# One matmul of 129 columns in place of 65 and 64 in a first layer's attention, with the low part added at eviction

## The chip, the cores and the metric

The kernel runs on one NeuronCore of a Trainium2 chip. The metric is the time of one execution on the device, in microseconds (us). Every matrix product is made of float16 pieces: a float32 value is split into a high float16 part and the float16 remainder (the "low" part), and three products (high by high, high by low, low by high) are summed in PSUM.

## The reference

Two layers act on 1024 latent tokens of width 1024 and 256 context tokens. The first is grouped-query attention: 16 query heads and 4 key/value heads of width 64, keys from latents and context together (1280 of them), then a SiLU gate and an output projection. The second is attention over a neighbourhood window. The change concerns the first layer alone:

```python
s = jnp.einsum('bqkgd,bskd->bkgqs', qi, k_all).astype(jnp.float32) * ATTN_SCALE
p = jax.nn.softmax(s, axis=-1).astype(v_all.dtype)
return jnp.einsum('bkgqs,bskd->bqkgd', p, v_all)
...
yx = (o * jax.nn.silu(z)) @ w_out
```

The changed lines compute the product of `p` and `v_all`, the division by the softmax sum, and the product with the gate.

## The kernel before

**Tiling.** Tokens are cut into tiles of 128: eight of latents, two of context. Layer one goes through eight units `u`, one for each pair of heads; a unit has three groups of query tiles `pt_`: two groups of four latent tiles, and one of the two context tiles. Inside a unit, `a_proj` (L944) makes queries and gates, `a_att` (L1177) the attention with keys on the partitions, and `q_att` (L1112) another form of the attention with queries on the partitions. For units 0 to 5 (`QH`) the second head of the latent groups goes through `q_att`; all else goes through `a_att`.

**One pass of `a_att`** is one head of one group. For a latent group it loops over the ten key tiles `kt`: two matmuls (L1204, L1205) put scores of 128 keys by 512 queries into a PSUM tile `st`; ScalarE takes the exponent twice, into float16 `ph` (L1189) and float32 `pf` (L1191); `p_split` (L1058) subtracts them, mostly on GpSimd, into the low part `pl`; `pv_mm` (L1068) multiplies with the values. `pv_mm` is called three key tiles late (`flush(3)`). A context group has two key tiles and two query tiles, and its exponents are named `phc` and `plc`.

**The values** lie in `v1[:, kt, g, :]` (L720), 130 float16 elements for each key tile and value head: 64 high values, one column of a constant (its product is the softmax sum), 64 low values from element 65 on. `pv_mm` issues three matmuls for each query tile: `ph` by the 65 columns of high values and constant (L1072), `ph` by the 64 low values into the same PSUM columns (L1073), `pl` by the 65 columns (L1074). The exponent tile is the stationary operand, so each matmul has a weight load (LDWEIGHTS, engine PEld) of its own.

**Eviction.** When the last key tile of a pass is in, `o_evict` (L1047) reads the PSUM tile `pv`: a reciprocal of the sums (L1050), a product with it (L1052), a product with the gate into `og` (L1054), all three on VectorE. `pv` has two buffers under one tag, which `q_att` uses for its `qpv` too: in units 0 to 5, `a_att` goes from pass to pass on one buffer while `q_att` holds the other. A pass can start its value matmuls only when its buffer has been read to the end.

**The order of the work** is not that of the code. `Planner` (L50) takes the recorded instructions with their dependences, prices each (`cost`, L93: a 65-column matmul at 30, a 64-column one at 34, longer ones at columns / 2.4 + 3), and places them engine by engine (`schedule`). `refine` (L468) repeats this with due times from the last order and keeps the order whose planned end is earliest. The orders of all engines are then fixed. An edit anywhere in layer one therefore moves instructions around it on every engine.

Of the kernel before, what the change touches and what calls it, by code (L numbers as in the profile page):

```python
# [16 lines left out]
ALU = mybir.AluOpType  # L17
# [4 lines left out]
P = 128  # L22
# [4 lines left out]
NT = NX + NC  # L27
TOK = NT * P
HD = 64
NH = 16  # L30
NKV = 4
EPS = 1e-6
# [477 lines left out]
def trunk_kernel(ctx, tc, x, cx, cc, ng_row, w_mod, w_mod0, b_mod, a_qz, a_kv, a_qg, a_kg, a_w_out,  # L510
                 b_in, tab, b_w_out, fin_g, ones, cos_t, sin_t, out):
    nc = tc.nc
    V, S, G, T, DM = nc.vector, nc.scalar, nc.gpsimd, nc.tensor, nc.sync
# [8 lines left out]
    def ps_tag(name, tag, dt=F32, shape=(P, 512)):  # L522
        return (psum if tag in ("pj", "pv") else psum1).tile(list(shape), dt, name=name, tag=tag, bufs=2)
# [8 lines left out]
        return ps_tag(name, "st")  # L532

    def ps_pv(name):
        return ps_tag(name, "pv", shape=(P, 4, 65))

    idf = main.tile([P, P], F32, name="idf")
    make_identity(nc, idf)
# [183 lines left out]
    G.memset(v1[:, :, :, 64:65], 2.0 * WS * WS)  # L722
    gcq = ap.tile([P, NX, HD], F32, name="gcq")
    gsq = ap.tile([P, NX, HD], F32, name="gsq")
    gcol = ap.tile([P, HD], F32, name="gq")
    gks = ap.tile([P, HD], F32, name="gk")

# [5 lines left out]
    def sq_tiles(pool):  # L733

        ts = [pool.tile([P, 4, HD + 1], F32, name=f"sq{j}", bufs=1) for j in range(2)]
        for s_ in ts:
            G.memset(s_[:, :, HD:HD + 1], HD * EPS * WS * WS)
        return ts
# [121 lines left out]
    for kt in range(KT):  # L860
# [8 lines left out]
        for t in ((0, 2) if kt < 2 else (0,)):  # L869
            n = 2 if kt < 2 else 4  # L870
# [56 lines left out]
    aq = apool2.enter_context(tc.tile_pool(name="aq", bufs=2))  # L927
    NPAIR = NH // 2

# [116 lines left out]

    def o_evict(pool, pv, og, n, sz, t0, i, nm):  # L1047

        rs = pool.tile([P, 4], F32, name="ors" + nm, tag="ors", bufs=2)
        V.reciprocal(rs[:, 0:n], pv[:, 0:n, 64])  # L1050
        hd = slice(i * HD, (i + 1) * HD)
        V.tensor_tensor(pv[:, 0:n, 0:HD], pv[:, 0:n, 0:HD], rs[:, 0:n].unsqueeze(2).broadcast_to([P, n, HD]),  # L1052
                        op=ALU.mult)
        V.tensor_tensor(og[:, 0:n, hd], pv[:, 0:n, 0:HD], sz[:, t0:t0 + n, hd], op=ALU.mult)  # L1054

    nsplit = [0]

# [10 lines left out]
    def pv_mm(pv, hi, lo, v, n, first, last):  # L1068

        for t in range(n):  # L1070
            c = slice(t * P, (t + 1) * P)
            T.matmul(pv[:, t, :], hi[:, c], v[:, 0:65], start=first and t == 0, stop=False)  # L1072
            T.matmul(pv[:, t, 0:HD], hi[:, c], v[:, 65:129], start=False, stop=False)  # L1073
            T.matmul(pv[:, t, :], lo[:, c], v[:, 0:65], start=False, stop=last and t == n - 1)  # L1074

    def o_out(pool, og, n, dst, u, nm):

# [99 lines left out]
    def a_att(u, pt_):  # L1177
# [18 lines left out]
        og = og_of(u, pt_)  # L1196
        for i in ((0,) if pt_ < 2 and u in QH else (0, 1)):
            pvs = ps_pv(f"pv{u}{i}{pt_}")
            if pt_ < 2:
                for kt in range(NT):  # L1200
                    st = ps_st(f"st{u}{i}{pt_}{kt}")
                    kc = slice(kt * P, (kt + 1) * P)
                    so = st.rearrange("p (t q) -> p t q", q=P)
                    T.matmul(so, k1[:, g, kc], q1[:, :, i, :], start=True, stop=False)  # L1204
                    T.matmul(so, k2[0:65, g, kc], q2[0:65, :, i, :], start=False, stop=True)  # L1205
                    ph, pl = p_tiles(st, f"{u}{i}{pt_}{kt}")
                    pend.append(lambda pvs=pvs, ph=ph, pl=pl, kt=kt: pv_mm(
                        pvs, ph, pl, v1[:, kt, g, :], 4, kt == 0, kt == NT - 1))
                    flush(3)
                    yield 800  # L1210
            else:
                st = ps_st(f"stc{u}{i}")
                for j in range(2):
                    kc = slice((NX + j) * P, (NX + j + 1) * P)
                    o = st[:, j * 256:(j + 1) * 256].rearrange("p (t q) -> p t q", q=P)
                    T.matmul(o, k1[:, g, kc], q1[:, :, i, :], start=True, stop=False)
                    T.matmul(o, k2[0:65, g, kc], q2[0:65, :, i, :], start=False, stop=True)
                ph, pl = p_tiles(st, f"c{u}{i}")

                def cpv(pvs=pvs, ph=ph, pl=pl):  # L1220
                    for j in range(2):
                        c = slice(j * 256, (j + 1) * 256)
                        pv_mm(pvs, ph[:, c], pl[:, c], v1[:, NX + j, g, :], 2, j == 0, j == 1)
                pend.append(cpv)
                yield 800

            def fin(pvs=pvs, i=i):
                o_evict(aq, pvs, og, n, sz, 0, i, f"{u}{i}{pt_}")
                og_done(u, pt_)
# [18 lines left out]
    first = 1.0  # L1248
# [102 lines left out]
    for t in range(4):  # L1351
        v = OV + OW * t
# [519 lines left out]
def _bias(rpb):  # L1872

    rp = np.pad(rpb.transpose(0, 2, 1), ((0, 0), (0, 0), (8, 8)))
    t = np.full((NH, P, 9, 8, GR), NEG, np.float32)
    t[:, :, 4:8] = 0.0
    for p in range(P):
# [7 lines left out]
        t[:, p, 3, 0:c, k] = v[:, 16:16 + c]  # L1885
    return t.reshape(NH, P, 9 * P)

# [54 lines left out]
```

## Time and profile before

| what | value |
|---|---|
| time, median of 3 runs | 1319.07 us (1318.21 to 1323.93) |
| profiled execution, its own time | 1312.96 us |
| span in that profile | 1311.2 us |
| granted TensorE clock | 0.999 |
| attention of layer one | about 130 to 690 us of the span |
| output projection of layer one begins | about 690 us |

A PE row is a matmul, a PEld row its weight load. Matmuls overlap in the records: a 65-column matmul is shown with about 193 ns, while the next one starts some 30 ns after it. The price of a matmul in a stream is therefore read from start to start, not from its duration.

### The profile page before, as it was taken

What the parts mean: (1) busy time and instruction counts of PE and PEld (TensorE: products, weight loads), DVE (VectorE), ACT (ScalarE), POOL (GpSimd) and SP (SyncE); (2) the same over time, 40 slices, a digit from 0 to 9 for tenths busy, and PEclk for the clock granted to TensorE, in tenths of its full rate; (3) what the DMA queues carried; (4) which work ended last, traced back from release to release, by engine and by line L of the source; (5) the groups of instructions that cost most, each with busy time, mean ns of one, the idle gap of its engine ahead of it and who ended that gap; (6) DMA issues with size and microseconds to landing.
All of it is one profiled execution on the core that took longest, in us unless ns stands there. A gap on an engine that the chain in (4) does not pass through costs nothing. (4 is left out here: it accounts for less than half of the span.)

```text
span 1311.2 us, 37092 instructions
## 1 busy us (share of the span) xinstructions
PE 1281.5 (98%) x14503; PEld 899.9 (69%) x14503; DVE 1025.2 (78%) x2410; ACT 893.9 (68%) x1835; POOL 807.4 (62%) x1030
## 2 busy tenths in 40 slices
PE   9999999999999999999999999999999999999997
PEld 6458777777777777767654466778696777868543
DVE  4787788798979798969658896778888788788743
ACT  3672797788878887778864345777878677777611
POOL 1572787677687876768864883556665555553432
PEclk9999999999999999999999999999999999999999
DMA  9422478778788886884406795789798887979923
GB/s 371 162 82 72 99 142 167 134 179 170 140 161 184 153 164 145 168 213 124 137 34 181 209 165 175 136 172 182 148 182 167 165 188 138 195 155 236 244 97 113
DMA packets 431610, 211.40 MB, mean 161 GB/s; under 512 B 386697, under 2 KB 390601, under 8 KB 431433
## 3 DMA queue, kind: packets, MB, share of 16 engines
q1 hardware_dynamic: 431434, 209.04, 71.4%
q8 instruction: 113, 1.85, 0.6%
q14 instruction: 63, 0.52, 0.1%
HBM read 97.23 MB, written 14.71 MB: 85 GB/s over the span
## 5 line engine op out<-in xcount | busy, mean ns | idle before, releaser
L1066 POOL TENSOR_TENSOR pl<-pf,ph 128x256 f16<-128x256 f32 x340 | 239.4, 728 | 66.6 <-ACT pf L1191 51.8
L1066 POOL TENSOR_TENSOR bph<-bpf,bph 128x256 f16<-128x256 f32 (+1 forms) x172 | 148.9, 890 | 184.4 <-ACT bpf L1640 122.9
L967 PE MATMUL pa<-wa,x 128*128 128x256 f16 x1536 | 216.5, 272 | 0.4 <-DVE mrow L626 0.2
L967 PEld LDWEIGHTS <-x 128*128 128x128 f16 x1536 | 141.8, 97 | 35.6 <-issue 1.8
L1189 ACT ACTIVATE ph<-st 128x512 f16<-128x512 f32 x200 | 118.7, 605 | 64.0 <-PE st L1205 53.3
L998 DVE TENSOR_REDUCE mxp<-pm 128x1 f32<-128x512 f32 x160 | 107.7, 683 | 14.6 <-PE pm L997 13.0
L1191 ACT ACTIVATE pf<-st 128x512 f32<-128x512 f32 x200 | 119.0, 610 | 0.2 <-POOL pl L1066 0.2
L1066 POOL TENSOR_TENSOR qpp<-qpf,qpp 128x512 f16<-128x512 f32 x84 | 96.4, 1168 | 30.0 <-ACT qpf L1148 23.2
L1639 ACT ACTIVATE bph<-bpf,bnx 128x640 f16<-128x640 f32 (+1 forms) x128 | 96.4, 794 | 26.6 <-DVE bnx L1634 25.9
L1505 PEld LDWEIGHTS <-wb 128*128 128x128 f16 x672 | 61.3, 98 | 68.1 <-issue 4.9
L1073 PE MATMUL pv<-v,ph 128*128 128x64 f16 x800 | 104.7, 195 | 0.0
L1072 PE MATMUL pv<-v,ph 128*128 128x65 f16 x800 | 104.1, 193 | 0.0
L1074 PE MATMUL pv<-v,pl 128*128 128x65 f16 x800 | 103.5, 192 | 0.1
L1640 ACT ACTIVATE bpf<-bpf,bnx 128x640 f32<-128x640 f32 (+1 forms) x128 | 101.3, 792 | 0.2
L1503 PEld LDWEIGHTS <-s 128*128 128x128 f16 x1536 | 87.0, 98 | 4.9 <-issue 3.7
L1072 PEld LDWEIGHTS <-ph 128*128 128x128 f16 x800 | 75.9, 97 | 19.9 <-issue 0.5
L1073 PEld LDWEIGHTS <-ph 128*128 128x128 f16 x800 | 75.5, 97 | 13.8 <-issue 0.2
L1074 PEld LDWEIGHTS <-pl 128*128 128x128 f16 x800 | 76.2, 99 | 9.4 <-POOL pl L1066 0.8
L1204 PE MATMUL st<-q,k 128*128 128x512 f16 x200 | 75.4, 379 | 3.8 <-ACT pf L1191 3.6
L1205 PE MATMUL st<-q,k 65*128 65x512 f16 x200 | 74.9, 380 | 3.1 <-DMA q<-zt 3.0
L1468 POOL TENSOR_TENSOR tsb<-wsb 128x256 f32<-128x256 f32 x64 | 52.5, 841 | 31.2 <-DMA wsb<-in_b_in 23.3
L1140 DVE CUSTOM_DVE_ANT_0 qpf<-qs,zero 128x512 f32<-128x512 f32 x96 | 65.6, 684 | 6.0 <-PE qs L1138 2.7
(549 smaller groups left out, 3889.4 us busy)
## 6 DMA issues: line engine op xcount, KB each, us to landing
wg<-in_w_mod SPq DMA_DIRECT2D x64, 256.0 KB
wsb<-in_b_in SPq DMA_DIRECT2D x64, 256.0 KB
tb<-in_tab SPq DMA_DIRECT2D x16, 576.0 KB
wm<-in_w_mod SPq DMA_DIRECT2D x16, 512.0 KB
wsa<-in_a_qz SPq DMA_DIRECT2D x32, 256.0 KB
xstage<-in_x SPq DMA_DIRECT2D x8, 512.0 KB
wsoa<-in_a_w_out SPq DMA_DIRECT2D x16, 256.0 KB
x<-in_x SPq DMA_DIRECT2D x8, 512.0 KB
```

The source lines that it names most:

```text
L967: T.matmul(ps[:, :, i, :], hA(a, kt, t), wt[w][:, kt, :], start=n == 0, stop=n == 3 * KT - 1)
L998: V.tensor_reduce(mxs[i][:, t, ch:ch + 1], pm, axis=AX.X, op=ALU.max)
L1066: G.tensor_tensor(lo[:, c], p32[:, c], hi[:, c], op=ALU.subtract)
L1072: T.matmul(pv[:, t, :], hi[:, c], v[:, 0:65], start=first and t == 0, stop=False)
L1073: T.matmul(pv[:, t, 0:HD], hi[:, c], v[:, 65:129], start=False, stop=False)
L1074: T.matmul(pv[:, t, :], lo[:, c], v[:, 0:65], start=False, stop=last and t == n - 1)
L1189: S.activation(ph, st, AF.Exp)
L1191: S.activation(p32, st, AF.Exp)
L1204: T.matmul(so, k1[:, g, kc], q1[:, :, i, :], start=True, stop=False)
L1503: T.matmul(ps[:, t], a_blk(a, kt, m)[:, t], w[kt][:, b, WIX[m]], start=f, stop=l, skip_group_check=not first)
L1639: S.activation(ph, pf[:, 0:k_], AF.Exp, bias=m)
L1640: S.activation(pf[:, 0:k_], pf[:, 0:k_], AF.Exp, bias=m, accum_out=sums[:, t - t0, i:i + 1])
```

## The change

Columns of `pv` are laid out anew: each query tile gets `VC` = 129 columns, in the order of `v1` (64 high, 1 sum, 64 low), as far as the bank of 512 columns goes. That holds three tiles of 129 and a fourth of 65. For the first three query tiles, one matmul of 129 columns replaces the pair of 65 and 64, and the product with the low values lands in columns of its own. The fourth tile keeps its three matmuls. Context groups have two query tiles, and both take the new form. At eviction ScalarE copies the low columns into `og`, VectorE adds them to the high ones in PSUM, and then the two products follow as before. `refine` gets 10 rounds for 5.

```diff
+VC = 2 * HD + 1
...
-        return ps_tag(name, "pv", shape=(P, 4, 65))
+        return ps_tag(name, "pv")
...
+        def cols(c, k, m):
+            a = pv[:, c:c + m]
+            return bass.AP(a.tensor, a.offset, [list(a.ap)[0], [VC, k], [1, m]])
+
         rs = pool.tile([P, 4], F32, name="ors" + nm, tag="ors", bufs=2)
-        V.reciprocal(rs[:, 0:n], pv[:, 0:n, 64])
-        hd = slice(i * HD, (i + 1) * HD)
-        V.tensor_tensor(pv[:, 0:n, 0:HD], pv[:, 0:n, 0:HD], rs[:, 0:n].unsqueeze(2).broadcast_to([P, n, HD]),
-                        op=ALU.mult)
-        V.tensor_tensor(og[:, 0:n, hd], pv[:, 0:n, 0:HD], sz[:, t0:t0 + n, hd], op=ALU.mult)
+        V.reciprocal(rs[:, 0:n].unsqueeze(2), cols(HD, n, 1))
+        hd, w = slice(i * HD, (i + 1) * HD), min(n, 3)
+        S.copy(og[:, 0:w, hd], cols(HD + 1, w, HD))
+        V.tensor_tensor(cols(0, w, HD), cols(0, w, HD), og[:, 0:w, hd], op=ALU.add)
+        o = cols(0, n, HD)
+        V.tensor_tensor(o, o, rs[:, 0:n].unsqueeze(2).broadcast_to([P, n, HD]), op=ALU.mult)
+        V.tensor_tensor(og[:, 0:n, hd], o, sz[:, t0:t0 + n, hd], op=ALU.mult)
...
-            c = slice(t * P, (t + 1) * P)
-            T.matmul(pv[:, t, :], hi[:, c], v[:, 0:65], start=first and t == 0, stop=False)
-            T.matmul(pv[:, t, 0:HD], hi[:, c], v[:, 65:129], start=False, stop=False)
-            T.matmul(pv[:, t, :], lo[:, c], v[:, 0:65], start=False, stop=last and t == n - 1)
+            c, o = slice(t * P, (t + 1) * P), pv[:, VC * t:VC * t + HD + 1]
+            f = first and t == 0
+            if t < 3:
+                T.matmul(pv[:, VC * t:VC * t + VC], hi[:, c], v[:, 0:VC], start=f, stop=False)
+            else:
+                T.matmul(o, hi[:, c], v[:, 0:HD + 1], start=f, stop=False)
+                T.matmul(o[:, 0:HD], hi[:, c], v[:, HD + 1:VC], start=False, stop=False)
+            T.matmul(o, lo[:, c], v[:, 0:HD + 1], start=False, stop=last and t == n - 1)
...
-        plan.refine(5, 100.0, 300.0)
+        plan.refine(10, 100.0, 300.0)
```

The added lines move what follows, so L1072 to L1074 of before are L1081 to L1085 of the changed kernel, and L967 is L968.

On PE, in the last key tile of the first pass of unit 4 (`pv400`: unit 4, head 0, group 0), two query tiles stand so before; `ph4009` and `pl4009` are the high and low exponents of that key tile:

```order
L1074 LDWEIGHTS pl4009_8019
L1074 MATMUL pv400_7541<-v1_125,pl4009_8019 128x65
L1072 LDWEIGHTS ph4009_8015
L1072 MATMUL pv400_7541<-v1_125,ph4009_8015 128x65
L1073 LDWEIGHTS ph4009_8015
L1073 MATMUL pv400_7541<-v1_125,ph4009_8015 128x64
```

The same place in the changed kernel:

```order
L1081 LDWEIGHTS ph4009_7757
L1081 MATMUL pv400_7301<-v1_125,ph4009_7757 128x129
L1085 LDWEIGHTS pl4009_7761
L1085 MATMUL pv400_7301<-v1_125,pl4009_7761 128x65
L1081 LDWEIGHTS ph4009_7757
L1081 MATMUL pv400_7301<-v1_125,ph4009_7757 128x129
```

One weight load and one matmul are gone for each of the first three query tiles. PE has 27595 rows before (a row is one or several equal instructions in a run) and 26267 after, 1328 fewer: 664 matmuls with their weight loads.

On VectorE (DVE), the eviction of that pass stands so before, from the reciprocal to the last product; the rows between belong to the next unit's queries (`pa`) and to row maxima (`mxp`, `qpf`):

```order
L1050 RECIPROCAL ors400_8137<-pv400_7541 128x4
L761 TENSOR_TENSOR pa51_7810<-pa51_7810,gsq_129 128x256
L1052 TENSOR_TENSOR pv400_7541<-pv400_7541,ors400_8137 128x4x64
L764 TENSOR_TENSOR pa51_7810<-t1q51_8078,pa51_7810 128x256
L998 TENSOR_REDUCE mxp500_7565<-pm50000_7952 128x1
L1140 ISA qpf403_7962,qmx403_7961<-qs4030_7964,zero_76 128x512
L1140 ISA qmx403_7961 128x1
L1054 TENSOR_TENSOR og40_7540<-pv400_7541,sz40_6115 128x4x64
```

And in the changed kernel:

```order
L1055 RECIPROCAL ors400_7867<-pv400_7301 128x4
L999 TENSOR_REDUCE mxp500_7325<-pm50011_7873 128x1
L776 TENSOR_TENSOR q16q51_7822<-pa51_7564,q16q51_7822 128x4x64
L1058 TENSOR_TENSOR pv400_7301<-pv400_7301,og40_7300 128x3x64
L1151 ISA qpf410_7951,qmx410_7950<-qs4100_7953,zero_76 128x512
L1151 ISA qmx410_7950 128x1
L1060 TENSOR_TENSOR pv400_7301<-pv400_7301,ors400_7867 128x4x64
L1155 TENSOR_REDUCE qnx403_7779<-qmx403_7706 128x1
L1005 TENSOR_REDUCE mxp500_7325<-pmc500_7957 128x2
L1061 TENSOR_TENSOR og40_7300<-pv400_7301,sz40_5935 128x4x64
```

The eviction has one VectorE row more (the addition, L1058), and other work stands between its rows: seven rows from the reciprocal to the last product before, nine after.

On ScalarE (ACT), the copy of the same pass has its place between exponents of the next pass (`ph4010`, `ph4011`):

```order
L974 ACTIVATE th52_8108<-pa52_7830 128x256
L775 CAST q16q51_7822<-pa51_7564 128x4x64
L1200 ACTIVATE ph4010_7940<-st4010_7937 128x512
L1057 COPY og40_7300<-pv400_7301 128x3x64
L1200 ACTIVATE ph4011_8018<-st4011_8015 128x512
```

Before, the two exponents follow each other there and nothing of the eviction is on ScalarE:

```order
L973 ACTIVATE th52_8379<-pa52_8091 128x256
L774 CAST q16q51_8083<-pa51_7810 128x4x64
L1189 ACTIVATE ph4010_8208<-st4010_8205 128x512
L1189 ACTIVATE ph4011_8286<-st4011_8283 128x512
L1191 ACTIVATE pf4010_8210<-st4010_8205 128x512
```

The copy stands behind one exponent and ahead of another. In layer two the order of each engine stays as it was, but for its first rows.

## The prediction

> **What bounds the kernel now.** I read the page first, then the busy times by stage, then who PE waits for in layer one. From the page, the span and the busy times of the engines:
>
> ```profile
> span 1311.2 us, 37092 instructions
> PE 1281.5 (98%) x14503; PEld 899.9 (69%) x14503; DVE 1025.2 (78%) x2410; ACT 893.9 (68%) x1835; POOL 807.4 (62%) x1030
> ```
>
> The windows of layer one's attention (130 to 690 us) and of all that follows. The first column after the window is its length, then PE, PEld, DVE, ACT and POOL busy, the granted clock, the DMA share and GB/s:
>
> ```profile
> 130.00:690.00 560.00, 545.26 (x6857) 406.33 (x6855) 455.62 (x1226) 440.05 (x903) 417.41 (x533) 1.00 0.69 147
> 690.00:1311.00 621.00, 610.69 (x6726) 412.18 (x6724) 477.72 (x961) 387.30 (x790) 336.45 (x418) 1.00 0.79 171
> ```
>
> PE is the bound, before and behind 690 us. In the attention it is idle 560.00 − 545.26 = 14.7 us, VectorE 104.4 us, ScalarE 120.0 us, and the granted clock is full. So each ns taken from PE's stream comes off the end, as long as the waits do not grow. The waits of PE in that stretch:
>
> ```profile
> PE qpv L1125 <- DMA qpt<-qpp: 5.2, 6, 1.1
> PE st L1204 <- ACT pf L1191: 3.6, 4, 2.1
> PE st L1205 <- DMA q<-zt: 3.0, 5, 1.0
> ```
>
> None of them is for a `pv` buffer. The instructions on the tile `pv` (durations are least, median and greatest, in ns), and the one wait for its eviction:
>
> ```profile
> L1072 PE MATMUL pv<-v,ph x800: 191/193/203, 131.6 to 681.9; 128*128 128x65 f16 x160
> L1072 PE MATMUL pv<-v,phc x64: 191/192/195, 191.7 to 688.5; 128*128 128x65 f16 x64
> L1050 DVE RECIPROCAL ors<-pv x36: 153/171/184, 155.9 to 688.8; 128x4 f32<-128x4 f32 x20, 128x2 f32<-128x2 f32 x16
> L1052 DVE TENSOR_TENSOR pv<-pv,ors x36: 283/417/433, 157.6 to 689.0; 128x256 f32<-128x256 f32 x20, 128x128 f32<-128x128 f32 x16
> ...
>   PEld L1072: 0.2, 1
> ```
>
> There are 20 latent passes of 4 query tiles (800 = 20 × 10 key tiles × 4) and 16 context passes of 2 (64 = 16 × 2 × 2).
>
> **What the change removes.** Three of four query tiles lose one matmul and its weight load, 600 sites; both context tiles do, 64 sites: 664 in all. The columns that stream through PE stay the same (65 + 64 + 65 = 129 + 65 = 194), so only the cost of an instruction by itself can go. I read it from start to start. In the timeline of PE, eight triples in a row, of 24 rows the first three and the last, and the matmul after them:
>
> ```profile
> 624.05 0.19 PE L1072 MATMUL pv<-v,ph 128*128 128x65 f16 x1
> 624.08 0.19 PE L1073 MATMUL pv<-v,ph 128*128 128x64 f16 x1
> 624.11 0.19 PE L1074 MATMUL pv<-v,pl 128*128 128x65 f16 x1
> ...
> 624.76 0.19 PE L1074 MATMUL pv<-v,pl 128*128 128x65 f16 x1
> 624.79 0.38 PE L997 MATMUL pm<-k,q 128*128 128x512 f16 x1
> ```
>
> A triple takes (624.79 − 624.05) / 8 = 92.5 ns. The nearest rows to the new pair of 129 and 65 columns are pairs of 128 and 64: in layer two ten pairs in a row (values that lie side by side), and in `q_att` eight pairs (values in two pieces, the second from element 65 on); the first rows and the row after the last:
>
> ```profile
> 835.88 0.22 PE L1647 MATMUL bpv<-bv,bpht 128*128 128x128 f16 x1
> 835.94 0.19 PE L1648 MATMUL bpv<-bv,bpht 128*128 128x64 f16 x1
> ...
> 836.73 0.33 PE L1588 MATMUL pv1c<-wb,hcx 128*128 128x128 f16 x3
> ```
>
> ```profile
> 301.26 0.22 PE L1125 MATMUL qpv<-v,qpt 128*128 128x128 f16 x1
> ...
> 301.95 0.19 PE L1074 MATMUL pv<-v,pl 128*128 128x65 f16 x1
> ```
>
> These take 0.85 / 10 = 85.0 ns and 0.69 / 8 = 86.3 ns. For two columns more I add 2 × 85.0 / 192 = 0.9 ns: 85.9 to 87.2, and take 86.5. A site saves 92.5 − 86.5 = 6.0 ns (5.3 to 6.6), and 664 sites save **4.0 us** (3.5 to 4.4).
>
> The triple is dearer than its columns say. Two 512-column matmuls in a row, with the work of PE around them at one eviction, where PE goes from unit 4's first pass to its second:
>
> ```profile
> 432.79 0.19 PE L1074 MATMUL pv<-v,pl 128*128 128x65 f16 x1
> 432.82 1.14 PE L967 MATMUL pa<-wa,x 128*128 128x256 f16 x9
> 433.80 0.38 PE L997 MATMUL pm<-k,q 128*128 128x512 f16 x1
> 434.01 0.38 PE L1137 MATMUL qs<-k,q 128*128 128x512 f16 x1
> 434.23 0.38 PE L1138 MATMUL qs<-k,q 65*128 65x512 f16 x1
> ...
> 436.66 0.19 PE L1072 MATMUL pv<-v,ph 128*128 128x65 f16 x1
> ```
>
> One of 512 columns takes 0.43 / 2 = 215 ns. With 85.0 for two matmuls of 192 columns together, a column costs (215 − 42.5) / (512 − 96) = 0.415 ns and an instruction 215 − 512 × 0.415 = 2.7 ns by itself. A triple would then be 194 × 0.415 + 3 × 2.7 = 88.6 ns, and it is 92.5: some 4 ns hang on one of its three matmuls. I take it that they go with the removed one, since both nearest pairs, one of which also reads from element 65 on, show nothing like it.
>
> The Trainium skill, "TensorE: Matmul & The Clock Gate", section "Wait — 56ns, not 53.3ns?", gives a matmul in a warm stream its columns / 2.4 GHz and about 2.5 ns fixed. The pairs of 85.0 ns agree with it (192 / 2.4 + 5 = 85.0), the triple does not (194 / 2.4 + 7.5 = 88.3). By that rule alone the change is worth 664 × 2.5 = 1.7 us where the rows say 4.0.
>
> **What it adds.** Each of 36 evictions gets a ScalarE copy and a VectorE addition, of 192 columns (20) or 128 (16). The nearest rows are the copy and the addition of `q_att`'s eviction, and an exponent for its greater width:
>
> ```profile
> L1170 ACT COPY qoc<-qpv x12: 347/367/408, 180.2 to 561.7; 128x256 f32<-128x256 f32 x12
> L1171 DVE TENSOR_TENSOR qoc<-qpv,qoc x12: 414/418/425, 181.6 to 564.0; 128x256 f32<-128x256 f32 x12
> L1189 ACT ACTIVATE ph<-st 128x512 f16<-128x512 f32 x200 | 118.7, 605 | 64.0 <-PE st L1205 53.3
> ```
>
> ScalarE: (605 − 367) / 256 = 0.93 ns a column, so 307 and 248 ns; 20 × 0.307 + 16 × 0.248 = 10.1 us. VectorE: 128 columns are the 283 ns of L1052's least, 192 lie between that and 418, about 351; 20 × 0.351 + 16 × 0.283 = 11.5 us. Against idle times of 120.0 and 104.4 us these lie beside PE's work and cost nothing by themselves. They could only bite through a queue (an exponent that stands behind the copy comes 0.3 us later, and PE waits for exponents 3.6 us now) or through the buffer.
>
> **The buffer.** The eviction grows by copy and addition, less the reciprocal that now runs beside the copy: 0.31 + 0.35 − 0.17 = 0.5 us; with an exponent of 0.6 us ahead of the copy on ScalarE, as in the order shown above, 1.1 us. The first value matmul of the next pass is queued behind that on PE, and with it everything later in PE's order. The eviction after the first of the two passes above, on VectorE:
>
> ```profile
> 433.02 0.18 DVE L1050 RECIPROCAL ors<-pv 128x4 f32<-128x4 f32 x1 [0.58 <-PE pv L1074]
> ...
> 435.43 0.42 DVE L1054 TENSOR_TENSOR og<-pv,sz 128x256 f32<-128x256 f32 x1
> ```
>
> The buffer is free at 435.85 and used at 436.66, 0.8 us to spare. So the old order could not carry a longer eviction everywhere; the new order must. I counted in PE's orders the work between the last matmul of a pass and the first of the pass that takes its buffer, priced as above (256 columns: 0.98 / 9 = 109 ns). Here it is 9 matmuls of 256 columns, 8 of 512 and 8 pairs before, 3.4 us; in the changed order 9, 10, 8 pairs and 16 short ones that I leave out, 3.8 us. Units 0 to 5 have 23 such places, with 4.1 us on average before and 5.2 us after, the short ones left out; they got longer at 17 of the 23. The 1.1 us that the gaps gain are what the eviction grows by, so I enter the buffer at **0**. If the cover were short, each 0.1 us at the 23 places would cost 2.3 us.
>
> **The order.** All engines' rows in layer one move by some places. Its waits of 14.7 us can shrink or grow; nothing read here gives a sign, so 0, with ± 3 us as an ordinary case.
>
> **The sum.** 1312.96 − 4.0 = 1309.0 for an execution like the profiled one. The median of the runs, 1319.07, lies 6.1 us above it with the same program, so the forecast against it is 1319.07 − 4.0 = **1315.0 us**, a gain of 0.3%. About 0.5% (6.6 us) is what a measurement of this kernel can tell from no change; this is less.
>
> **The rivals.**
>
> *The new order also removes waits.* For it: 14.7 us of idle PE in layer one is a stock to take from, its largest waits are for transposes and exponents whose place in the queues is what the order sets, and twice the rounds give it more to choose from. Against it: the waits are where the chip ran later than planned, and more rounds do not know of that. With 40% gone it gives 4.0 + 5.9 = 9.9 us less, 1309.2 us.
>
> *The buffer becomes the wait (slower).* For it: two buffers, a tight turn of 0.8 us, a copy on another engine behind exponents. Against it: more PE work in each gap, and 0.2 us of such waits now. It outweighs the gain once a turn is late by 4.0 / 23 = 0.17 us on average, and shows as slower beyond 0.5% from 10.6 / 23 = 0.46 us on. At half of the 1.1 us it costs 23 × 0.55 = 12.7, less 4.0: 1327.7 us.
>
> *Only the fixed cost goes.* If the 4 ns hang on reading the low values, wherever they are read, they stay in the matmul of 129 columns and a site saves 2.7 ns: 664 × 2.7 = 1.8 us, 1317.3 us. For it: the row in the triple that costs more may be the one with the low values. Against it: the pair at 86.3 ns reads such values with 1.3 ns more, not 4. The rule of the Trainium skill cited above ("TensorE: Matmul & The Clock Gate") comes out on this side, 1.7 us.
>
> **How the numbers follow.** The forecast gets 0.46, the removed waits 0.27, the buffer 0.14, the fixed cost alone 0.13. Faster by over 0.5% are the second case and a little of the first (0.03): 0.30. Slower is the third: 0.14. The same: 0.43 + 0.13 = 0.56. The likeliest case alone spans 1312 to 1318. The range reaches down past the removed waits (half of them gone: 1319.07 − 4.0 − 7.4 = 1307.7) and up into the buffer's case (0.4 us at each turn: 1319.07 − 4.0 + 9.2 = 1324.3): 1307 to 1325.
>
> **What would show it.** Right: 664 matmuls fewer on PE, a 129-column matmul followed by a 65-column one every 86 to 87 ns, PE's idle time in the attention near 15 us, and layer one's output projection starting about 4 us earlier with everything behind it shifted alike. The second case: that idle time near 9 us. The buffer: waits of the 129-column matmul, or its weight load, for the last product of the eviction or for the copy, several us in all. The fixed cost alone: pairs every 90 ns instead. Wrong altogether: a pair as dear as the triple, or a change in layer two.

## The result, and the profile after

The changed kernel takes **1310.33 us** (median of 4 runs, 1309.54 to 1314.83), the kernel before 1319.96 us (4 runs, 1318.21 to 1323.93): a ratio of 0.9943, 95% interval 0.9920 to 0.9966, or 7.5 us less (4.5 to 10.6). The prediction had 1315.0 us with a range of 1307 to 1325. The time lies in the range, 4.7 us below the forecast and nearest to the rival of the removed waits (1309.2).

The two profiled executions can't be set beside each other as they are: that of before is its fastest run (1312.96 us), that of after its slowest (1314.83). From the page of after, the span and the busy times:

```profile
span 1313.1 us, 35823 instructions
PE 1281.4 (98%) x13839; PEld 898.4 (68%) x13839; DVE 1031.0 (79%) x2446; ACT 902.3 (69%) x1871; POOL 801.8 (61%) x1030
```

PE has 14503 − 13839 = 664 matmuls and as many weight loads fewer, VectorE and ScalarE have 36 instructions more each. The busy sum of PE hardly moves (1281.5 before), since it counts overlapping matmuls until their ends. The same two windows as of before, with the same columns (length, then PE, PEld, DVE, ACT and POOL busy, clock, DMA share, GB/s):

```profile
130.00:690.00 560.00, 542.44 (x6176) 401.65 (x6175) 458.30 (x1251) 446.29 (x936) 415.33 (x533) 1.00 0.70 147
690.00:1313.00 623.00, 612.95 (x6735) 413.62 (x6733) 480.52 (x969) 387.99 (x791) 333.38 (x418) 1.00 0.79 171
```

PE is idle for 560.00 − 542.44 = 17.6 us of the attention; before it was 14.7. Nothing was taken from the waits there. Who PE waits for in that stretch:

```profile
PE qpv L1136 <- DMA qpt<-qpp: 7.5, 8, 2.2
PE st L1215 <- ACT pf L1202: 5.7, 8, 2.8
PE st L1216 <- DMA q<-zt: 1.4, 2, 1.0
```

The same causes lead, and none is the `pv` buffer. The instructions on the tile `pv` (least, median and greatest duration in ns), and at the end the one wait for its eviction:

```profile
L1081 PE MATMUL pv<-v,ph x600: 217/220/300, 130.7 to 681.8; 128*128 128x129 f16 x150
L1055 DVE RECIPROCAL ors<-pv x36: 152/170/183, 156.3 to 691.1; 128x4 f32<-128x4 f32 x20, 128x2 f32<-128x2 f32 x16
L1057 ACT COPY og<-pv x36: 246/312/380, 156.9 to 691.3; 128x192 f32<-128x192 f32 x20, 128x128 f32<-128x128 f32 x16
L1058 DVE TENSOR_TENSOR pv<-pv,og x36: 281/354/367, 157.6 to 692.0; 128x192 f32<-128x192 f32 x20, 128x128 f32<-128x128 f32 x16
...
  PEld L1081: 0.6, 1
```

Copy and addition have the medians of 312 and 354 ns that the prediction had worked out as 307 and 351. In 36 evictions a weight load for a value matmul waits once, 0.6 us. The spacing of the new pairs, in PE's timeline (start, duration, engine, line, operation), four pairs of a context group and the matmul after them:

```profile
623.00 0.22 PE L1081 MATMUL pv<-v,phc 128*128 128x129 f16 x1
623.05 0.19 PE L1085 MATMUL pv<-v,plc 128*128 128x65 f16 x1
...
623.32 0.19 PE L1085 MATMUL pv<-v,plc 128*128 128x65 f16 x1
623.34 0.38 PE L1215 MATMUL st<-q,k 128*128 128x512 f16 x1
```

Four pairs in 0.34 us are 85 ns each within the rounding of the rows. Over the whole trace, a pair takes 86.80 ns from its start to the start of what follows (mean of 489, stalls left out), a triple of before 92.76 ns (mean of 687): 5.96 ns less, and 664 × 5.96 = 4.0 us. That is the predicted term. It leaves 7.5 − 4.0 = 3.5 us to be explained, with an uncertainty of 3 us.

### The profile page after: what moved, and what is told of

Its sections match the earlier page's. It is cut to its first block, busy times and chain, and to the rows that moved or that the text cites. A ratio compares the mean times of both kernels' runs of the same rounds, so it can differ in the third digit from the quotient of the medians.

```text
span 1313.1 us, 35823 instructions
## 1 busy us (share of the span) xinstructions
PE 1281.4 (98%) x13839; PEld 898.4 (68%) x13839; DVE 1031.0 (79%) x2446; ACT 902.3 (69%) x1871; POOL 801.8 (61%) x1030
## 3 DMA queue, kind: packets, MB, share of 16 engines
q8 instruction: 108, 1.77, 0.6%
## 4 chain that ended last, share of the span: by engine, by line
PE 78%; DVE 8%; DMA 7%; ACT 3%; issue 2%; POOL 1%; SPq 1%; POOLq 0%; DVEq 0%; ACTq 0%
PE pa L968 10%; PE poa L1308 8%; PE pob L1812 5%; PE pkv L835 4%; PE bsa L1632 4%; DMA qpt<-qpp 3%; PE bpv L1658 2%; PE st L1215 2%; PE st L1216 2%; PE pv L1081 2%; DMA bpht<-bph 2%; PE pm L998 2%; DVE mxp L999 1%; PE pv L1085 1%; PE qpv L1136 1%
## 5 line engine op out<-in xcount | busy, mean ns | idle before, releaser
L1073 POOL TENSOR_TENSOR pl<-pf,ph 128x256 f16<-128x256 f32 x340 | 235.2, 716 | 72.3 <-ACT pf L1202 60.1
L968 PE MATMUL pa<-wa,x 128*128 128x256 f16 x1536 | 216.8, 273 | 0.0
L968 PEld LDWEIGHTS <-x 128*128 128x128 f16 x1536 | 144.5, 98 | 37.5 <-issue 1.4
L1085 PE MATMUL pv<-v,pl 128*128 128x65 f16 x800 | 99.6, 193 | 0.2 <-POOL pl L1073 0.2
L1514 PEld LDWEIGHTS <-s 128*128 128x128 f16 x1536 | 87.7, 98 | 3.3 <-issue 2.1
L1081 PE MATMUL pv<-v,ph 128*128 128x129 f16 x600 | 88.8, 221 | 0.0
L1085 PEld LDWEIGHTS <-pl 128*128 128x128 f16 x800 | 73.8, 98 | 20.0 <-issue 3.3
L1658 PE MATMUL bpv<-bv,bpht 128*128 128x128 f16 x608 | 67.2, 220 | 2.3 <-DMA bpht<-bph 2.1
L1308 PE MATMUL poa<-woa,oar 128*128 128x512 f16 x288 | 68.8, 379 | 0.0
L1812 PE MATMUL pob<-wob,obr 128*128 128x512 f16 (+2 forms) x306 | 67.1, 367 | 0.8 <-DVE bmx L1640 0.8
```

The lines of the kernel that those rows point to most:

```text
L968: T.matmul(ps[:, :, i, :], hA(a, kt, t), wt[w][:, kt, :], start=n == 0, stop=n == 3 * KT - 1)
L1073: G.tensor_tensor(lo[:, c], p32[:, c], hi[:, c], op=ALU.subtract)
L1081: T.matmul(pv[:, VC * t:VC * t + VC], hi[:, c], v[:, 0:VC], start=f, stop=False)
L1085: T.matmul(o, lo[:, c], v[:, 0:HD + 1], start=False, stop=last and t == n - 1)
L1308: T.matmul(ps, lhs(a, kt), w[b][:, kt, :], start=n == 0, stop=n == 3 * KT - 1)
L1812: T.matmul(ps, ob[kt][:, t // 4, a, c], wob[kt, hf][:, b, wc], start=n == 0, stop=n == 3 * KT - 1)
```

## The experiments

The theory after the result: the streaming gives 4 us whatever the order, the longer eviction costs nothing in the new order, and the rest comes from the new order of the work. Rivals: the added rounds of the planner did it; the odd start of the low values (element 65) is what the old triple paid for; the order has nothing to do with it and the merge is worth all 7.5 us.

### Rounds alone

The kernel before with the changed kernel's rounds, and the changed kernel with those of before:

```diff
-        plan.refine(5, 100.0, 300.0)
+        plan.refine(10, 100.0, 300.0)
```

> The kernel before with 10 rounds of the planner's refinement for 5, and nothing else changed; its order differs from that of before in layer one. Theory A (the gain of the change is the streaming of 664 fewer matmuls, some 4.4 us, and the rest is the order that more rounds found): 0.997 to 0.998 of before, 2.5 to 4 us less, with less idle time of PE between 130 and 690 us. Theory B (the whole gain comes with the merged matmuls, the rounds do nothing): 1.000 within 0.15%.

1318.17 us, ratio 1.0004 (0.9989 to 1.0019): the rounds alone do nothing for the kernel before, although its order is another one. That is theory B's figure, and theory A's (0.997 to 0.998) is out.

> The changed kernel with 5 rounds as before: merged matmuls and the longer eviction alone. Theory A: 0.9965 of before, 4.4 us less. Theory B: 0.994, as the whole change. Theory C (the longer eviction costs something, and the rounds make up for it): 0.998 or more.

1314.14 us, ratio 0.9976 (0.9964 to 0.9988), 3.2 us less than before. With 5 rounds the change is worth about its streaming term; with 10, 7.5 us. Theory B (0.994) is out here; theory A (0.9965) and the first figures of theory C (0.998 or more) both lie in the interval.

### The low values at an even element

```diff
-    v1 = ap.tile([P, NT, NKV, 130], F16, name="v1")
+    v1 = ap.tile([P, NT, NKV, 132], F16, name="v1")
...
-            T.matmul(pv[:, t, 0:HD], hi[:, c], v[:, 65:129], start=False, stop=False)
+            T.matmul(pv[:, t, 0:HD], hi[:, c], v[:, 66:130], start=False, stop=False)
```

> The kernel before with the low values moved from element 65 to element 66 of each row of values (rows of 132 elements), so that the 64-column matmul starts its read at a multiple of 4 bytes. The order of every engine stays what it was. If the 4 to 5 ns by which a triple is dearer than its columns hang on the start of that read: triples at about 88 ns, 864 sites by 4.5 ns is 3.9 us less, 0.997 of before. If they hang on something else (the third matmul on the same PSUM columns, the same weights loaded twice): triples at 92.5 ns and 1.000.

1316.96 us, ratio 0.9997 (0.9981 to 1.0013). A triple takes 92.05 ns in place of 92.76 (means of 682 and 687): 0.7 ns of the excess of 4 hang on the odd start, not the rest (864 triples by 0.7 ns are 0.6 us). Every engine has the order of before, so this is also a second profile of that order, and one that lies at its own median (1317.09 us).

### The change again

> The changed kernel again, beside the same runs of before as the three others. All theories: 0.994 of before, 7 to 8 us less.

1309.13 us, ratio 0.9931 (0.9909 to 0.9953), and its profiled execution took 1309.22 us. This and the run before it, both profiled at their medians, are the pair to compare. The time in us at which the first value matmul of layer one, the first matmul of layer two's line L1503 (L1514 after the change) and the first of its output projection (L1801, L1812) start in each trace:

| run | first value matmul | layer two | last projection | span |
|---|---|---|---|---|
| order of before (low values at 66) | 131.69 | 769.00 | 1214.05 | 1315.3 |
| the change | 130.86 | 763.00 | 1206.07 | 1307.4 |
| difference | −0.8 | −6.0 | −8.0 | −7.9 |

Of the gain, 6.0 us are there when layer two begins, and 2.0 us come between that point and the last projection. In the waits of PE between 770 and 790 us, at the start of layer two, the order of before has one line (us in total, times, longest):

```profile
PE pv0y L1503 <- ACT e L1524: 1.7, 1, 1.7
```

This wait is in both profiles of that order and in none of the three of the change. On ScalarE, the copy that PE waits for stands behind two casts there, ahead of which ScalarE waits 1.35 and 0.24 us for VectorE; in the change one cast stands in its place and waits for nothing. It belongs to the order that the planner makes: all three orders of the triples (3, 5 and 10 rounds) have the 1.7 us, the merged kernels in the order of before have 1.3 us (both below), and no order that was planned for the pairs has it. The second place is near 585 us. In the order of before with the low values at 66, PE's wait there, ScalarE's wait ahead of it (both between 570 and 592 us), and the windows after it, in which the granted clock stands third from the end:

```profile
PE st L1204 <- ACT pf L1191: 3.2, 1, 3.2
```

```profile
ACT woa L678 <- DMA wsoa<-in_a_w_out: 3.9, 1, 3.9
```

```profile
585.00:590.00 5.00, 2.61 (x17) 1.67 (x17) 3.13 (x7) 4.88 (x10) 1.30 (x2) 0.62 0.48 163
590.00:595.00 5.00, 5.00 (x45) 3.28 (x44) 2.39 (x5) 2.99 (x7) 2.86 (x3) 0.69 0.44 132
```

ScalarE stands still for a weight transfer of the output projection, exponents come late, and PE waits 3.2 us. From 586.2 us on, still within that wait, the granted clock is at half for 6.8 us. PE is busy for 5.7 of them, so 2.8 us are lost. The change in the run of the table, where the wait is shorter:

```profile
PE st L1215 <- ACT pf L1202: 1.4, 1, 1.4
```

```profile
585.00:590.00 5.00, 5.00 (x63) 3.83 (x62) 4.39 (x10) 4.95 (x12) 4.32 (x6) 1.00 0.66 224
```

The clock stays full. Streaming (4.0, less the 0.6 that the even start had saved already), the wait in layer two (1.7), the shorter wait here (3.2 − 1.4 = 1.8) and the clock behind it (2.8) make 9.7 of gain, where the spans differ by 7.9. The other 1.8 us are only in part to be seen: waits for transposes grew by 1.3 (6.4 against 5.1), but PE's idle time in the attention fell from 16.4 to 14.8 us, so all waits but the one near 585 us grew by 0.2 together. The clock's part comes and goes between runs of one program. The profile of before happens to have the clock full throughout layer one, and from it to this run of the change the span shrinks by only 1311.2 − 1307.4 = 3.8 us.

### The matmul taken apart again, in the order of the change

The lines left out price the two matmuls as the one and keep them together:

```diff
...
-                T.matmul(pv[:, VC * t:VC * t + VC], hi[:, c], v[:, 0:VC], start=f, stop=False)
+                T.matmul(o, hi[:, c], v[:, 0:HD + 1], start=f, stop=False)
+                T.matmul(pv[:, VC * t + HD + 1:VC * t + VC], hi[:, c], v[:, HD + 1:VC], start=False, stop=False)
```

> The changed kernel with each 129-column matmul taken apart again into 65 and 64 columns, the 64 into the same columns of their own, and with every engine's order held as in the changed kernel (the second matmul is priced at nothing and kept behind the first). Eviction and layout are those of the change. Theory A (streaming of 664 matmuls is worth 4.0 to 4.4 us, the rest came with the order): 4.0 to 4.4 us above the changed kernel, 0.996 to 0.997 of before. Theory B (it is the order alone, or the shorter stream only turns into waits): as the changed kernel, 0.9935. And on why a triple takes 92.5 ns and not 88.6: 92 or more here if it is that three short matmuls, each with a weight load, stand in a row; 88 to 89 if it was that the third added onto columns just written.

1315.72 us, ratio 0.9986 (0.9972 to 1.0000). Four triples at the place whose pairs are shown above:

```profile
624.05 0.19 PE L1092 MATMUL pv<-v,phc 128*128 128x65 f16 x1
624.08 0.20 PE L1093 MATMUL pv<-v,phc 128*128 128x64 f16 x1
624.11 0.19 PE L1097 MATMUL pv<-v,plc 128*128 128x65 f16 x1
...
624.39 0.19 PE L1097 MATMUL pv<-v,plc 128*128 128x65 f16 x1
624.42 0.38 PE L1227 MATMUL st<-q,k 128*128 128x512 f16 x1
```

0.37 / 4 = 92.5 ns, and 92.71 as the mean of 490, although the low part goes to columns of its own here. The excess of the triple is thus not a matter of adding into the same PSUM columns either.

### The eviction cut short

The lines left out keep the planner's prices, and with them the order:

```diff
...
-        S.copy(og[:, 0:w, hd], cols(HD + 1, w, HD))
-        V.tensor_tensor(cols(0, w, HD), cols(0, w, HD), og[:, 0:w, hd], op=ALU.add)
+        S.copy(og[:, 0:w, i * HD:i * HD + 1], cols(HD + 1, w, 1))
+        V.tensor_tensor(cols(0, w, 1), cols(0, w, 1), og[:, 0:w, i * HD:i * HD + 1], op=ALU.add)
```

> The changed kernel with the eviction's copy and addition cut to one column for each query tile, in the same order on every engine; 63 of 64 low columns are left out of the sum. Theory A (the longer eviction is covered): within 0.1% of the changed kernel. Theory C (the buffer or the ScalarE queue costs something): 1.5 us or more below the changed kernel, 0.992 or less of before.

1308.79 us, ratio 0.9939 (0.9921 to 0.9957), beside the change a third time, on the same chip:

> The changed kernel again on this chip, to which the two others are compared: 0.993 to 0.9945 of before.

1309.77 us, ratio 0.9947 (0.9928 to 0.9967). In the new order the longer eviction costs 1.0 us by the medians, which is not to be told from nothing, nor from the 1.5 us at which theory C begins (by the ratios 1.1 us, −2.4 to 4.6). From the split to the whole matmul, with the order held, the ratios give 0.9986 − 0.9947 = 0.0039, 5.1 us, with 2 to 8 us as the interval (root of the summed squares of the two half-widths). The spacing, 92.71 − 86.81 = 5.90 ns, gives 3.9 us. The difference agrees with theory A's 4.0 to 4.4 us, and theory B (none) is out, although theory A's ratio for the split kernel (0.996 to 0.997) lies just outside the interval that was measured. And the new order without the merge is worth 1.8 us (0 to 3.7).

### Another order of the change

```diff
-        plan.refine(10, 100.0, 300.0)
+        plan.refine(8, 100.0, 300.0)
```

> The changed kernel with 8 rounds of refinement, whose order is neither that of 5 rounds nor that of 10 (the order of 9 rounds, which 10 and 20 keep). If orders differ on the chip by chance, anywhere from 0.992 to 0.999 of before; if later rounds are steadily better on the chip, between 0.9976 and 0.9935.

1306.41 us, ratio 0.9922 (0.9900 to 0.9943). The order of 8 rounds, which the planner thought worse than the one it kept, has the lowest median of all kernels here. It lies in the band of chance, and outside that of steadily better rounds.

### The change in the order of before

The planner orders the program of before; that order is laid on the changed program. The core of the edit (`old.start` and `old.done` are planned starts and ends; the copy is placed at the planned end of the reciprocal or, if that is later, of the last use of the tile that was in its buffer; five passes keep the old form, so 618 sites are merged):

```diff
+        order = {e: [to[j] for j in o if j in to] for e, o in old.order.items()}
+        at = {to[j]: old.start[j] for j in to}
+        for c, j in extra:
+            t = old.done[j - 1]
+            for name in old.came.get(j + 1, ()):
+                t = max([t] + [old.done[u] for u in old.tiles[name][2]])
+            at[c] = t
+            order["DVE"].insert(order["DVE"].index(to[j]), c + 1)
+        order["ACT"] = sorted(order["ACT"] + [c for c, _ in extra], key=at.__getitem__)
```

> The change in the order of before: the planner orders the program of before with its 5 rounds, and that order is laid on the changed program, instruction by instruction; the removed matmuls drop out, the addition stands directly ahead of the product with the reciprocal on VectorE, and the copy stands on ScalarE at the planned end of the reciprocal. Five of the 36 passes (four context ones, one latent) keep the old form, because their output tile is still in use there: 618 sites are merged in place of 664. Theory (the streaming and the order are two terms that add, and the eviction has room): 618 x 6.2 ns = 3.8 us faster than before, about 1313.5 us, ratio 0.997, waits of PE for the eviction below 1 us in all. Rival (the old order has no room for a longer eviction, as the 0.8 us to spare at one turn says): at 23 turns an eviction that is up to 0.5 us longer, plus the time that the copy waits behind an exponent, brings waits of the 129-column matmul for the last product of 2 to 10 us in all, and a time of 1316 to 1324 us, ratio 0.999 to 1.005.

1318.17 us, ratio **1.0001** (0.9987 to 1.0014). The pairs take 86.92 ns here too, so 618 × 5.84 = 3.6 us were saved, and by the time all of it was given back: it is the rival's time. Places where PE waits longer stand in the timelines of PE and its weight loads, as idle time and what ended it (the last bracket):

```profile
413.01 0.10 PEld L1136 LDWEIGHTS <-ph 128*128 128x128 f16 x1 [1.25 <-DVE og L1109]
```

```profile
412.81 0.38 PE L1034 MATMUL pm<-k,q 128*128 128x512 f16 x1 [0.77 <-DVE qmx L1206]
```

```profile
PE pm L1034 <- DVE mxp L1035: 2.4, 4, 0.8
PE pm L1034 <- DVE qmx L1206: 1.0, 2, 0.8
```

L1109 is the eviction's last product: the next pass waits for its buffer. Weight loads of value matmuls do so four times, 2.8 us in all. L1034 (L997 of before) waits six times for row maxima on VectorE, 3.4 us in all where the kernel before has 0.5; at four of the six, VectorE did an addition in the 2.5 us before. The two sums don't give the whole account: a 65-column matmul is shown for some 190 ns while the next one starts 30 ns after it, so shorter waits don't show as idle time. In the kernel before, the waits of L997 for row maxima, and the only wait for a `pv` buffer:

```profile
PE pm L997 <- DVE mxp L998: 0.5, 1, 0.5
```

```profile
619.86 0.10 PEld L1072 LDWEIGHTS <-phc 128*128 128x128 f16 x1 [0.18 <-DVE og L1054]
```

The same kernel with the short eviction (the copy and addition of one column, as above):

> The kernel of the run before this one with the copy and the addition cut to one column for each query tile (63 of 64 low columns are left out of the sum), in the same order. Theory (the eviction has room): the same time as the full eviction within 1 us, about 1313.5 us, ratio 0.997. Rival (no room): 2 to 8 us faster than the full eviction. If the streaming gain needs the new order, both kernels stay at 1317.5 us, ratio 1.000.

1313.48 us, ratio 0.9981 (0.9962 to 1.0001). Its weight loads at the same turn and its waits for maxima:

```profile
409.31 0.10 PEld L1136 LDWEIGHTS <-ph 128*128 128x128 f16 x1 [0.40 <-DVE og L1109]
```

```profile
PE pm L1034 <- DVE mxp L1035: 1.4, 3, 0.7
```

The waits shrink, those of the weight loads for the buffer from 2.8 to 1.5 us and those of L1034 from 3.4 to 1.4. By the ratios 2.6 us come back, by the medians 4.7; that is the rival's forecast (2 to 8 us), but the intervals of the two ratios overlap, so the time alone doesn't settle it, and the rows show the place. The 2.5 us (0 to 5) by which this kernel is faster than before can't be told from the 3.6 of streaming.

### Two more orders

The change with 3 rounds, and the kernel before with 3 rounds:

> The change with 3 rounds of the planner, another order again. If what an order is worth is chance, the time lies anywhere in the band of the other orders of the change, ratios 0.990 to 0.999 (5 rounds gave 0.9976, 8 gave 0.9922, 10 gave 0.993 to 0.995). If more rounds are what removes the waits, 3 rounds are slower than 5: ratio 0.998 or more.

1317.81 us, ratio 0.9996 (0.9980 to 1.0013): 0.998 or more, as for rounds that remove waits, and just above the band of chance.

> The kernel before with 3 rounds of the planner: its matmuls and evictions as they are, in another order. Theory (an order by itself moves the time by some us, with or without the change): a ratio between 0.994 and 1.004, and 1.000 as with 10 rounds is as likely as a difference. Rival (only the changed program has better orders to find, because its evictions leave more room or PE more slack): 1.000 to 1.004 and nothing faster. A ratio below 0.995 would mean that most of what the change gained could have come from the order alone.

1313.01 us, ratio 0.9966 (0.9952 to 0.9979): another order alone makes the kernel before 4.5 us faster (2.8 to 6.3), about as much as the merge by itself. All orders together, as ratios to the kernel before:

| order | triples | pairs |
|---|---|---|
| of before (5 rounds) | 1.0000 | 1.0001 (618 sites) |
| of the change (10 rounds) | 0.9986 | 0.9943, 0.9931, 0.9947 |
| other orders of the triples: 10, 3 rounds | 1.0004, 0.9966 | |
| other orders of the pairs: 3, 5, 8 rounds | | 0.9996, 0.9976, 0.9922 |

From one order to another the triples spread over 0.0038 (5.0 us) and the pairs over 0.0079 (10.4 us), where one ratio is known to about ± 0.002. More rounds are not a rule: with the pairs, 3, 5, 8 and 10 rounds give 0.9996, 0.9976, 0.9922 and 0.994, better up to 8; without the change 3, 5 and 10 give 0.9966, 1.0000 and 1.0004, the other way.

For the pairs, what an order is worth goes roughly with PE's idle time in the attention (560 us less PE's busy time from 130 to 690 us, one profile of each run, three of the change):

| order of the pairs | ratio | PE idle there, us |
|---|---|---|
| 8 rounds | 0.9922 | 12.3 |
| 10 rounds (the change) | 0.9943, 0.9931, 0.9947 | 17.6, 14.8, 15.2 |
| 5 rounds | 0.9976 | 18.4 |
| 3 rounds | 0.9996 | 18.0 |
| of before | 1.0001 | 17.9 |

The 17.6 belong to the run of 1314.83 us, the slowest of its four. The triples have 14.4 to 16.4 us in five profiles, and there the idle time does not rank the orders.

## Why the prediction was right or wrong

**The bound** held. PE is busy 98% before and after, and what PE was spared showed in the time where nothing took it back.

**Streaming** was right in size: 5.96 ns a site where 6.0 were entered, 4.0 us in all, and 5.1 us (2 to 8) by the times with the order held. Behind the choice stood that the 4 ns by which a triple is dearer than its columns would go with the removed matmul. They did, and this was the right side of the rival "only the fixed cost goes". The reason is neither the odd start (0.7 ns) nor adding into the same columns (none). In the kernel with the matmul taken apart, the middle one takes 33.7 ns from start to start, the first 29.8, the third 29.2 (means of the 490): it is the 64-column matmul between two others, each with its own weight load. Its width is not the reason: in layer two's pairs the 64-column matmul behind one of 128 takes 28.3 ns (L1648 of before, mean of 604). Why it is the dear one stays open. The rule of the Trainium skill, "TensorE: Matmul & The Clock Gate", section "Wait — 56ns, not 53.3ns?" (columns / 2.4 GHz and about 2.5 ns each), gives, as an estimate, the pair 194 / 2.4 + 5 = 85.8 ns, where 86.8 were measured, and the triple 88.3 ns, where it was 92.8. For short matmuls in a row the rows decide, and the 1.7 us by that rule were too few.

**Copy and addition** were right in size (312 and 354 ns) and, in the order that the planner made for them, in their price of 0: cutting both to one column changes the time by 1.0 us, within what can't be told from nothing.

**The buffer** was right for the reason given. The prediction read a turn with 0.8 us to spare, and said that the old order could not carry a longer eviction everywhere and the new one must. With the change in the old order, the time is that of before: the eviction takes back what the streaming gave. It does so at fewer turns than the 23 that were counted (weight loads of value matmuls wait for it four times, 0.4 to 1.25 us), and as much through a queue that the prediction didn't name. It named ScalarE's exponents; here the additions on VectorE push back the row maxima that PE's next matmuls wait for.

**The order** is the step that failed. It was entered at 0 with ± 3 us, "its waits of 14.7 us can shrink or grow", all inside layer one. By the split kernel the order alone gives 1.8 us (0 to 3.7). Streaming and order together are 4.0 + 1.8 = 5.8 of the measured 7.5 us (4.5 to 10.6), and the rest is within the uncertainty. Two things were missed. First, the place: against the profile of before, the waits inside the attention did not shrink (17.6 us idle, 14.8 and 15.2 in the change's other profiles, 14.7 before), so the rival that came nearest in time did not come true by its mechanism. Only against the merged kernel in the order of before (17.9 us idle) do two of those three profiles have 3 us less. What went is a wait of 1.7 us at the start of layer two, where the prediction had named a change as a sign of being wrong altogether, and in the run at the median the longer stop near 585 us with the half clock behind it. So it was not 4 us early in layer one with all behind it shifted alike: in that run layer two begins 6.0 us earlier, and 2.0 more come behind it. Second, the spread: orders of one program differ by 5 to 10 us here, so ± 3 was too narrow a case for it. That the time lies in the range is owed to its lower end, which was drawn for waits that go inside the attention; that about as much came off in other places is luck. How much of an order's worth lies in such stops, and how often each order meets them, can't be told from one profile of a run.

**The 6.1 us** between the median of before and its profiled execution were left unexplained. That execution was the fastest seen until then and free of the half clock near 585 us (a wait of 2.1 us there); the second profile of the same order, at its median, has a wait of 3.2 us there and loses 2.8 us by the clock. These 1.1 + 2.8 = 3.9 us are near the 4.1 by which its span is longer (1315.3 and 1311.2), and 3.1 of them are there when layer two begins (769.00 and 765.88 us). The other 2 us stay open.

## What to carry to other kernels

Price short matmuls in a stream from start to start, in the company in which they run: three of 64 or 65 columns cost 6 ns more than the same columns in two, and that held in every order tried. Where a planner fixes the order, an edit's own worth is smaller than the spread between orders (here 4 against 5 to 10 us): hold the order while measuring the edit, lay the old order under the new program as well, and then try several orders of the one that is kept. Of the kernels here the change with 8 rounds is the fastest, 1306.41 us.

## What the runs showed of the hardware

A wait of PE of 2 to 4 us in a busy kernel can cost 1.6 to 3.2 us more, because the granted clock then goes to half for 3.4 or 6.8 us. In the profile of the change, such a wait in layer two (between 1020 and 1032 us) and the windows that hold the half clock near 580 and after 1030 us:

```profile
PE bpv L1658 <- DMA bpht<-bph: 2.0, 1, 2.0
```

```profile
580.00:585.00 5.00, 4.14 (x36) 2.92 (x36) 3.83 (x6) 4.33 (x10) 4.11 (x5) 0.66 0.82 273
1030.00:1035.00 5.00, 4.62 (x50) 3.60 (x51) 1.73 (x5) 0.00 (x0) 5.00 (x11) 0.66 0.63 132
```

This execution has three such windows of 3.4 us inside the kernel (at 55.0, 580.7 and 1031.3 us), the change in the profile of 1309.22 us none, and the two spans are 5.7 us apart (1313.1 and 1307.4). The window at 55.0 left nothing behind: the first value matmul starts at 130.69 us here and at 130.86 there. Through the other two PE is busy for 6.7 us, which costs 3.3 us at half clock, and the waits ahead of them are 1.4 and 0.3 us longer than there (2.8 and 1.4 us, 2.0 and 1.7 us). Together that is 5.0 of the 5.7 us.

Whether a wait is followed by it is not settled by its length. Near 580 us, waits of 0.4 to 2.0 us never were, waits of 2.8, 3.2 and 3.6 us always, and of those from 2.1 to 2.4 us three were (2.1, 2.2, 2.4) and two not (2.1, 2.3). The records of the clock say what settles it. In each of the 14 traces of this case, the times between two changes of the clock are whole multiples of 3.413 us, so the changes lie on a grid of windows of that length. Between 20 and 1295 us the traces have 5180 such windows at full clock. All 11 with 1.90 us or more of idle PE were followed by half clock; of the 7 with 1.77 to 1.88 us three were; of the others none. A half-clock window with 0.39 us or more of idle PE was followed by a second one (3 of 3), one with 0.16 us or less never was. The two waits of 2.1 us differ in this: that of the kernel before lies across two windows, and in the first PE is idle for 3.41 − 2.03 = 1.38 us; that of its order of 3 rounds lies within one, with 3.41 − 1.32 = 2.09 us. First the window of before, then that of 3 rounds:

```profile
582.54:585.95 3.41, 2.03 (x28) 1.54 (x26) 1.71 (x4) 1.87 (x4) 0.02 (x1) 1.00 0.86 264
582.75:586.16 3.41, 1.32 (x17) 0.93 (x16) 1.20 (x5) 2.29 (x6) 0.54 (x1) 1.00 0.59 230
```

Several short waits in one window do as well: the window ahead of 55.0 us has 1.77 us of idle time, and its longest wait is 1.05 us. The Trainium skill, "TensorE: Matmul & The Clock Gate", section "What's actually happening", has the clock watched in free-running windows of about 3.4 us and halved after an idle one: the grid and the lengths of 3.4 and 6.8 us agree with it, but here a window that was idle for little more than half was enough.

The spread between runs of one program (8 us and more for the kernel before) is this in part. In 93 runs of the kernel before, beside which the experiments were measured, the mean time is 1315.6 us at a mean granted clock of 0.999 (21 runs) and 1318.7 us at 0.996 (14 runs); but at 0.999 alone the runs lie between 1312.7 and 1319.7 us, so most of the spread has another cause, which stays open.
